# The first norm's modulation in a two-layer hybrid backbone: float32 weights kept in TensorE, two conditions moved past them, x loaded first

## The chip, the core and the metric

The kernel runs on one core of a Trainium2 chip. A core has five engines that run side by side: TensorE (matmuls, called PE in the profile; PEld is the load of its weights), VectorE (DVE), ScalarE (ACT), GpSimd (POOL) and SyncE (SP), which here issues most DMA transfers. Data stand in SBUF (128 partitions), matmul results in PSUM, inputs and outputs in HBM. TensorE has two clock levels, 1.2 and 2.4 GHz; the profile shows the granted clock as a share of the higher one (0.50 or 1.00). The metric is the device time of one launch in microseconds, the median of several runs.

## What is computed

Two layers of a diffusion backbone for 128 context tokens and 512 latent tokens, D = 1024. Each layer is a token mixer (layer 0: a gated short convolution; layer 1: a two-way state-space scan) followed by a product-key expert layer. All of it is float32. What the change touches is the first norm of layer 0, with a shift and a scale that come from a condition vector, one for the context (`c_ctx`) and one for the latents (`c`):

```python
def run_trunk(x, cond, ...):
    for i in range(DEPTH):
        mod = (jax.nn.silu(cond) @ ada_w[i] + ada_b[i])[:, None, :]
        sh_a, scl_a, gt_a, sh_f, scl_f, gt_f = jnp.split(mod, 6, axis=-1)
        hn = rmsnorm(x, norm_mix_g[i]) * (1 + scl_a) + sh_a
        mix = short_conv_mixer(hn, ...)          # layer 0
        x = x + gt_a * mix
        ...

def short_conv_mixer(h, w_in, conv_w, w_out, grid):
    bg, cg, xv = jnp.split(h @ w_in, 3, axis=-1)
    return (bg * dwconv3(cg * xv, conv_w, grid)) @ w_out
```

`sh_a` and `scl_a` are the first 2048 of the 6144 columns of `silu(cond) @ ada_w[0]`. Only these are needed before the first projection.

## The kernel before

Activations lie with channels on the partitions: x is 8 tiles (k = 0..7) of 128 channels by 640 tokens (512 latent, 128 context). A float32 product of the large kind is done in three matmuls of a faster format: each operand is split into a high part (a copy on ScalarE, `Stream.high` L89 or `split` L120) and the rest (a subtraction on VectorE, L98 or L121), and `mm3` (L123 to L127) adds high x high, high x low and low x high.

The first 70 us of the program go through these stages.

- `run` (L143) loads the small vectors, makes `sl` = silu(cond) for both conditions (128 x 8 x 2) and splits it into `silu` (four columns per k).
- `ada` (L220) computes the shift and the scale. Its 16 weight tiles of 0.52 MB come through a `Stream` (tag "a": raw `ar`, high `ah`, low `al`). Here the condition is the stationary operand (four columns, a high and a low one per condition) and the weights move past it, 512 columns a matmul, into `arow` (L232, L233). A row of four results is copied to `arows` (L237), and four small float32 matmuls against `sel` (L242) add high and low and turn the row into columns, in `apm`; ScalarE copies them to `mod` (L243), and `modulated` (L269) adds the bias and makes `gs` = (1 + scale) times the norm's weight. This is done for four parts of 512 columns. `ada` is a generator; `conv_layer` steps it at fixed places among the other instructions.
- x is loaded on the same SP queue, after the first five `ar` tiles (L412).
- `stat` (L283) squares each tile of x on ScalarE (`sq`), adds them up on VectorE, and matmuls with `ones` give the sums `st` (L294). `rstd` (L310) turns these into the norm's factor `rs`, with five transposes `rb` (L319).
- `norm` (L322) makes for each k: `nt` = x * rs on VectorE (L327), times `gs` plus shift on ScalarE for each of the two token groups (L329), and the split into `chi` and `clo` (L120, L121).
- The conv layer's loop over j (8 channel tiles of each of the three projections): `cg`, `xv` and `bg`, each 48 matmuls of 320 columns (16 of `mm3`'s triples). For j = 0 `cg` and `xv` run with `rows=True`: k is the outer loop, so a k is used as soon as its tile is there. Their weights come through the stream `win` (raw `wr`, high `wh`, low `wl`). Beside the loop VectorE computes the other modulation parts (`modulation`, L247), two multiply-and-sum steps for each 128 columns.

The order within an engine is set by a scheduler of the language, which sorts the instructions by its own model of time from the order in the code; only the expert layers have an order written out by hand. Each engine then takes its instructions strictly in that order and waits where an operand isn't there. Tiles with a name and `bufs=n` share n buffers in turn.

Of the kernel before, what the change touches and what calls it, by code (L numbers as in the profile page):

```python
# [9 lines left out]
F32 = mybir.dt.float32  # L10
F32R = mybir.dt.float32r
# [4 lines left out]
AF = mybir.ActivationFunctionType  # L16
ALU = mybir.AluOpType
# [4 lines left out]
P = 128  # L22
NL = 512
# [4 lines left out]
KT = 8  # L28
D = 1024
# [12 lines left out]
START = 4  # L42
# [71 lines left out]
class K:  # L114
# [28 lines left out]
    def run(s):  # L143
        nc, A = s.nc, s.A
        with ExitStack() as ctx:
# [24 lines left out]
            s.silu = c.tile([P, KT, 4], F32R, name="silu")  # L170
            for n in range(2):
                s.split(s.silu[:, :, 2 * n], s.silu[:, :, 2 * n + 1], sl[:, :, n])
            s.sel = c.tile([4, 2], F32, name="sel")
            nc.sync.dma_start(s.sel, A["sel"])
# [45 lines left out]
    def ada(s, parts, pool, ps, loads=3):  # L220

        nc = s.nc
        st = Stream(s, pool, [s.A["ada_w"][n, q] for _, n in parts for q in range(4)], "a", loads, 2)
        st.prime()
        for e, (i, n) in enumerate(parts):
            row = ps.tile([P, 512], F32, name="arow", tag="arow", bufs=1)[:4]
            for q in range(4):
                wh, wl = (t.rearrange("p a b -> p (a b)").rearrange("p (a b) -> p a b", a=2)
                          for t in st.get(4 * e + q))
                for k in range(2):  # L230
                    c = s.silu[:, 2 * q + k, :]
                    nc.tensor.matmul(row, c, wh[:, k, :], start=(q + k == 0), stop=False)  # L232
                    nc.tensor.matmul(row, c, wl[:, k, :], start=False, stop=(q + k == 4))  # L233
                if q < 3:
                    yield True
            r = pool.tile([4, 512], F32, name="arows", bufs=2)
            nc.scalar.activation(r, row, AF.Copy)  # L237
            yield True
            yield True
            pm = ps.tile([P, NL], F32, name="apm", tag="apm", bufs=1)[:, :8].rearrange("p (a b) -> p a b", b=2)  # L240
            for m in range(4):
                nc.tensor.matmul(pm[:, m, :], r[:, m * P:(m + 1) * P], s.sel, start=True, stop=True)  # L242
            nc.scalar.activation(s.mod[i][:, 4 * n:4 * n + 4], pm, AF.Copy)  # L243
            s.modulated(i, n)
            yield True
# [148 lines left out]
    def conv_layer(s):  # L394
        nc, A = s.nc, s.A
        with ExitStack() as ctx:
            big = s.pool(ctx, "cbig")
            tmp = s.pool(ctx, "ctmp", bufs=2)
            win = Stream(s, s.W, [A["sc_w_in"][m] for m in range(24)], "w")
            wout = Stream(s, s.W, [A["sc_w_out"][m] for m in range(8)], "w")  # L400
            hi = big.tile([P, KT, NT], F32R, name="chi")
            lo = big.tile([P, KT, NT], F32R, name="clo")
# [4 lines left out]
            ps = s.pool(ctx, "cps", space=PSUM)  # L407
            ax = ExitStack()
            mods = s.ada([(0, n) for n in (2, 0, 3, 1)], s.pool(ax, "cada"), ps, START)
            next(mods)  # L410
            for k in range(KT):
                nc.sync.dma_start(s.x[:, k, :], A["xT"][:, k, :])  # L412
            for _ in range(11):
                next(mods)
# [4 lines left out]
            with ExitStack() as nx:  # L419
                tp = s.pool(nx, "normtmp")  # L420
                for _ in mods:
                    pass
                win.prime()
                s.norm(0, 0, hi, lo, tp)
# [947 lines left out]
def lay(I):  # L1372
# [4 lines left out]
    A = {}  # L1377

    def mt(w):

        k, n = w.shape[0] // P, w.shape[1] // P
        return np.ascontiguousarray(w.reshape(k, P, n, P).transpose(2, 1, 0, 3).reshape(n, P, k * P))
# [6 lines left out]
    def col(v):  # L1389
# [11 lines left out]
    A["ada_w"] = np.ascontiguousarray(  # L1401
        w[0, :, :2048].reshape(4, 2, P, 4, 512).transpose(3, 0, 2, 1, 4)).reshape(4, 4, P, D)
    A["ada_wT"] = np.ascontiguousarray(w.transpose(0, 2, 1)).reshape(2, 48, P, D)
    A["sel"] = np.repeat(np.eye(2, dtype=np.float32), 2, axis=0)
# [46 lines left out]
```

## Time and profile before

| | |
|---|---|
| median of 3 runs | 4118.25 us (4109.04 to 4119.88) |
| profiled execution | 4117.18 us, its span 4115.5 us |
| TensorE busy | 4000.5 us (97% of the span) |
| VectorE busy | 3414.4 us (83%) |
| ScalarE busy | 1661.4 us (40%) |
| mean granted clock | 0.987 |

The span is what the profiler sees from the first to the last instruction; the execution's time has 1.7 us more around it. Busy shares are means over stages of very different kind: the first 50 us, which the change touches, are one eightieth of the span, and there TensorE has gaps and a lower clock. So the rows to read are those of the stage, not of the whole. A matmul's duration in a row is longer than its distance from the next, since matmuls are pipelined; prices of matmuls in a row are taken from the distances. "[idle before <-releaser]" at a row's end tells how long the engine had waited and for whom.

### The profile page before, as it was taken

Reading aid. Unit: us, or ns where it says so; the run is one execution under the profiler, and the core shown is the slowest. Engines: PE = TensorE matmul, PEld = TensorE weight load, DVE = VectorE, ACT = ScalarE, POOL = GpSimd, SP = SyncE. Lnnn points to the kernel's source line nnn. Section 1 sums busy time; section 2 is a strip of 40 time slices with the busy share of each in tenths; the row PEclk is TensorE's granted clock in tenths of the full one; section 3 lists DMA queues with packets and bytes.
Section 4 is the critical chain, followed back from the end, with each engine's and each line's share of the span. In section 5 each row is a group of like instructions: output and inputs, shape, how many; then the busy total and the mean of one; then the engine's idle time right before and its main releaser. Section 6 shows DMA issues by size and latency. Waiting matters only on the chain.

```text
span 4115.5 us, 59000 instructions
## 1 busy us (share of the span) xinstructions
PE 4000.5 (97%) x22253; PEld 3543.9 (86%) x22253; DVE 3414.4 (83%) x6324; ACT 1661.4 (40%) x3060; POOL 421.6 (10%) x535
## 2 busy tenths in 40 slices
PE   8999999999999999999999999999999999999998
PEld 6999978788888888888999998987878888888887
DVE  7979997678788888878999867998858878888886
ACT  5233234433333333336555644223443333333332
POOL 0000000001111111111010100000001111111110
PEclk8999999999999999999999999999999999999999
DMA  6643238888888888963333234224888889998894
GB/s 218 219 159 109 81 131 248 266 307 321 313 316 324 322 322 322 327 249 123 118 102 119 85 128 148 94 86 161 249 280 300 323 316 325 323 323 321 323 324 181
DMA packets 344807, 957.33 MB, mean 233 GB/s; under 512 B 30091, under 2 KB 192139, under 8 KB 302537
## 3 DMA queue, kind: packets, MB, share of 16 engines
q1 hardware_dynamic: 147914, 514.53, 36.5%
q0 software_dynamic: 52224, 338.36, 22.1%
q10 hardware_dynamic: 144384, 100.67, 7.7%
q8 instruction: 174, 2.85, 0.3%
q14 instruction: 111, 0.91, 0.1%
HBM read 839.34 MB, written 114.04 MB: 232 GB/s over the span
## 4 chain that ended last, share of the span: by engine, by line
issue 41%; PE 32%; DVE 14%; POOL 8%; ACT 2%; DMA 2%; ACTq 1%; POOLq 0%; SPq 0%; DVEq 0%
POOL uv L587 8%; PE pact L125 3%; PE pact L126 3%; PE pact L127 3%; PE pj L125 2%; PE pj L126 2%; PE pj L127 2%; DVE ul L98 1%; DVE wl L98 1%; PE pg L978 1%; DMA uv<-uv,cidx 1%; PE pg L979 1%; DVE pr L825 1%; DVE idx L799 1%; DVE scr L795 1%
## 5 line engine op out<-in xcount | busy, mean ns | idle before, releaser
L125 PE MATMUL pact<-hnh,uh 128*128 128x480 f32 x2048 | 789.7, 386 | 12.7 <-ACT ga L508 9.4
L127 PE MATMUL pact<-hnh,ul 128*128 128x480 f32 x2048 | 781.7, 382 | 9.6 <-DVE ul L98 9.4
L126 PE MATMUL pact<-hnl,uh 128*128 128x480 f32 x2048 | 784.1, 383 | 0.0
L125 PE MATMUL acc<-h,wh 128*128 128x480 f32 x1536 | 584.6, 381 | 0.0
L127 PE MATMUL acc<-h,wl 128*128 128x480 f32 x1536 | 581.7, 379 | 0.0
L126 PE MATMUL acc<-h,wh 128*128 128x480 f32 x1536 | 581.7, 379 | 0.0
L89 ACT ACTIVATE wh<-wr 128x1024 fp32r<-128x1024 f32 x385 | 404.8, 1052 | 398.1 <-DMA wr<-uv 105.1
L98 DVE TENSOR_TENSOR wl<-wr,wh 128x1024 fp32r<-128x1024 f32 x385 | 469.7, 1220 | 59.4 <-ACT wh L89 58.3
L587 POOL DMA_INDIRECT uv<-uv,cidx x320 | 335.7, 1049 | 1661.8 <-DVE cacc L604 1540.1
L125 PEld LDWEIGHTS pact<-hnh,uh 128*128 128x128 f32 x2048 | 387.0, 189 | 76.1 <-ACT ga L508 13.1
L127 PEld LDWEIGHTS pact<-hnh,ul 128*128 128x128 f32 x2048 | 386.5, 189 | 74.0 <-DVE ul L98 13.6
L594 DVE SCALAR_TENSOR_TENSOR uv<-uv,hrow 128x1024 f32<-128x1024 f32 x320 | 390.8, 1221 | 57.3 <-DMA uv<-uv,cidx 55.6
L126 PEld LDWEIGHTS pact<-hnl,uh 128*128 128x128 f32 x2048 | 386.5, 189 | 58.3
L604 DVE SCALAR_TENSOR_TENSOR cacc<-uv,dg,cacc 128x1024 f32<-128x1024 f32 x316 | 405.1, 1282 | 0.0
L508 ACT ACTIVATE ga<-pact 128x480 f32<-128x480 f32 x256 | 145.6, 569 | 626.3 <-PE pact L127 626.0
L98 DVE TENSOR_TENSOR ul<-ur,uh 128x1024 fp32r<-128x1024 f32 x256 | 312.3, 1220 | 88.7 <-ACT uh L89 88.2
L89 ACT ACTIVATE uh<-ur 128x1024 fp32r<-128x1024 f32 x256 | 269.0, 1052 | 252.5 <-DMA ur<-uT 111.2
L581 DVE TENSOR_TENSOR h<-h,h 128x480 fp32r<-128x480 f32 x256 | 168.5, 658 | 197.0 <-PE rot L126 196.5
L127 PEld LDWEIGHTS acc<-h,wl 128*128 128x128 f32 x1536 | 289.1, 188 | 46.1
L126 PEld LDWEIGHTS acc<-h,wh 128*128 128x128 f32 x1536 | 289.1, 188 | 44.1
L125 PEld LDWEIGHTS acc<-h,wh 128*128 128x128 f32 x1536 | 289.4, 188 | 43.1
L596 ACT ACTIVATE dg<-dg 128x1 f32<-128x1 f32 x320 | 63.9, 200 | 422.3 <-DVE uv L594 422.3
(342 smaller groups left out, 8004.8 us busy)
## 6 DMA issues: line engine op xcount, KB each, us to landing
ur<-uT SPq DMA_DIRECT2D x256, 512.0 KB
wr<-uv SPq DMA_DIRECT2D x256, 512.0 KB
gdram<-st ACTq DMA_DIRECT2D x30, 2048.0 KB
gt<-gdram SPq DMA_DIRECT2D x62, 960.0 KB
mw<-ada_wT SPq DMA_DIRECT2D x80, 512.0 KB
adram<-ga ACTq DMA_DIRECT2D x128, 240.0 KB
ga<-adram SPq DMA_DIRECT2D x128, 240.0 KB
wr<-ssd_w SPq DMA_DIRECT2D x48, 512.0 KB
```

The source lines that it names most:

```text
L89: s.K.nc.scalar.activation(hi.rearrange("p a b -> p (a b)"), s.raw[s.nh], AF.Copy)
L98: s.K.nc.vector.tensor_sub(lo.rearrange("p a b -> p (a b)"), s.raw.pop(s.ns), hi.rearrange("p a b -> p (a b)").bitcast(F32))
L125: mm(out, wh, mh, start=start, stop=False)
L126: mm(out, wh, ml, start=False, stop=False)
L127: mm(out, wl, mh, start=False, stop=stop)
L508: nc.scalar.activation(g, pa, AF.Gelu)
L581: nc.vector.tensor_sub(h2, h, h1.bitcast(F32))
L587: nc.gpsimd.indirect_dma_start(out=t[:], out_offset=None, in_=A["uv"].rearrange("l e d -> (l e) d"), in_offset=bass.IndirectOffsetOnAxis(a ...
L594: nc.vector.scalar_tensor_tensor(UV[n][:, :D], UV[n][:, :D], 1.0, rows[n >= NX], op0=ALU.mult, op1=ALU.mult, accum_out=dg[:, n:n + 1])
L596: nc.scalar.activation(dg[:, n:n + 1], dg[:, n:n + 1], AF.Gelu)
L604: nc.vector.scalar_tensor_tensor(cacc, t[:, D:], dg[:, n:n + 1], cacc, op0=ALU.mult, op1=ALU.add)
L795: nc.vector.match_replace(scr[:, t], v[:, t, :8], src[:, t], imm_value=-3e38)
```

## The change

The weights of the first 2048 columns are laid out like other weights, 16 tiles of 128 columns with all eight k-parts in each. They stay float32 and unsplit, and now they are the stationary operand: for each 128 columns, eight matmuls with a 128 x 128 piece in the array and the two columns of `sl` moving past it, straight into columns of `apm`. `sel`, `silu`, `arow` and `arows` are gone. For each k the shift (tile k) and the scale (tile 8 + k) are done together (`first_mod`), followed by the norm of that k alone. x is loaded ahead of all weight tiles; these have six buffers, three pairs. The stream `win` is started in the turn of k = 4.

```diff
-    def ada(s, parts, pool, ps, loads=3):
+    def first_load(s, k, pool):
+        out = []
+        for m in (k, KT + k):
+            w = pool.tile([P, KT, P], F32, name="aw", bufs=AHEAD)
+            s.nc.sync.dma_start(w.rearrange("p a b -> p (a b)"), s.A["ada_w"][m])
+            out.append(w)
+        return out
+
+    def first_mod(s, k, ws, ps):
         nc = s.nc
...
-                    nc.tensor.matmul(row, c, wh[:, k, :], start=(q + k == 0), stop=False)
-                    nc.tensor.matmul(row, c, wl[:, k, :], start=False, stop=(q + k == 4))
...
+        pm = ps.tile([P, NL], F32, name="apm", tag="apm", bufs=1)[:, :4].rearrange("p (a b) -> p a b", b=2)
+        for a, w in enumerate(ws):
+            for q in range(KT):
+                nc.tensor.matmul(pm[:, a, :], w[:, q, :], s.sl[:, q, :], start=(q == 0), stop=(q == KT - 1))
+        for a in range(2):
+            m = KT * a + k
+            nc.vector.tensor_add(s.mod[0][:, m], pm[:, a], s.sv("adab", 2, 48)[:, 0, m:m + 1].to_broadcast([P, 2]))
+        nc.vector.scalar_tensor_tensor(s.gs[0][:, 0, k], s.mod[0][:, KT + k], 1.0,
+                                       s.sv("nmg", 2, KT)[:, 0, k:k + 1].to_broadcast([P, 2]),
+                                       op0=ALU.add, op1=ALU.mult)
...
-            mods = s.ada([(0, n) for n in (2, 0, 3, 1)], s.pool(ax, "cada"), ps, START)
-            next(mods)
+            ap = s.pool(ax, "cada")
             for k in range(KT):
                 nc.sync.dma_start(s.x[:, k, :], A["xT"][:, k, :])
-            for _ in range(11):
-                next(mods)
+            aw = {k: s.first_load(k, ap) for k in range(AHEAD // 2)}
...
                 tp = s.pool(nx, "normtmp")
-                for _ in mods:
-                    pass
-                win.prime()
-                s.norm(0, 0, hi, lo, tp)
+                for k in range(KT):
+                    s.first_mod(k, aw.pop(k), ps)
+                    if k + AHEAD // 2 < KT:
+                        aw[k + AHEAD // 2] = s.first_load(k + AHEAD // 2, ap)
+                    if k == 4:
+                        win.prime()
+                    s.norm(0, 0, hi, lo, tp, ks=[k])
```

AHEAD is 6. What this does to the order on the engines is seen at three places. On TensorE, from the last transpose of `rb` on, the order before has the last modulation part and then the first projections; `cg_472` and `cg_473` are the two halves of the tokens, and so `xv_536` and `xv_537`:

```order
L233 MATMUL arow<-al,silu 4x512
L125 MATMUL cg_472<-chi,wh 128x320
L125 MATMUL cg_473<-chi,wh 128x320
L126 MATMUL cg_472<-clo,wh 128x320
L127 MATMUL cg_472<-chi,wl 128x320
L126 MATMUL cg_473<-clo,wh 128x320
L127 MATMUL cg_473<-chi,wl 128x320
L242 MATMUL apm<-sel,arows 128x2 x4
L125 MATMUL xv_536<-chi,wh 128x320
L126 MATMUL xv_536<-clo,wh 128x320
```

The program's first matmuls on TensorE now, up to the same place (L230 is the new modulation matmul, L286 the sums, L311 the transposes of `rs`, L426 the later conditions' rows):

```order
L230 MATMUL apm<-sl,aw 128x2 x16
L286 MATMUL st<-ones,sq 128x64 x10
L230 MATMUL apm<-sl,aw 128x2 x16
L311 MATMUL rb<-ident,rt 128x128 x4
L230 MATMUL apm<-sl,aw 128x2 x8
L311 MATMUL rb<-ident,rt 128x128
L426 MATMUL srow<-ident,sl 128x128 x4
L230 MATMUL apm<-sl,aw 128x2 x88
L426 MATMUL srow<-ident,sl 128x128 x4
L125 MATMUL cg_455<-chi,wh 128x320
L126 MATMUL cg_455<-clo,wh 128x320
L125 MATMUL cg_456<-chi,wh 128x320
```

Before, the projections of the first k stand ahead of the last modulation part's turn into columns, and `xv` follows at once, mixed with `cg`; now all 128 modulation matmuls stand ahead of the first `cg`, and all of `cg` ahead of `xv`. On ScalarE, the copy `wh` of the first projection's weights stood ahead of the first scaled `nt`:

```order
L237 ACTIVATE arows<-arow 4x512
L89 ACTIVATE wh<-wr 128x1024
L243 ACTIVATE mod_92<-apm 128x8
L89 ACTIVATE ah<-ar 128x1024
L329 ACTIVATE nt<-nt,mod_92,gs_94 128x512
L89 ACTIVATE ah<-ar 128x1024
L329 ACTIVATE nt<-nt,mod_92,gs_94 128x128
```

and at the end of the norm there is now, on ScalarE:

```order
L321 ACTIVATE nt<-nt,mod_85,gs_87 128x128
L120 ACTIVATE chi<-nt 128x640
L427 ACTIVATE silurow<-srow 128x512
L321 ACTIVATE nt<-nt,mod_85,gs_87 128x512
L89 ACTIVATE wh<-wr 128x1024
L321 ACTIVATE nt<-nt,mod_85,gs_87 128x128
L427 ACTIVATE silurow<-srow 128x512
L120 ACTIVATE chi<-nt 128x640
```

The first `wh` has moved from ahead of the first `nt` to behind the first half of the last one (the last `chi` is the eighth). On SP the loads start so before:

```order
L158 DMA sm<-small 128x306
L160 DMA cnd<-condT 128x16
L174 DMA sel<-sel 4x2
L81 DMA ar<-ada_w 128x1024 x5
L412 DMA x<-xT 128x640 x8
L81 DMA ar<-ada_w 128x1024 x9
```

and now, on the same queue:

```order
L158 DMA sm<-small 128x306
L160 DMA cnd<-condT 128x16
L403 DMA x<-xT 128x640 x8
L220 DMA aw<-ada_w 128x1024 x16
L81 DMA wr<-sc_w_in 128x1024 x2
```

x has moved ahead of all modulation weights, and the first projection's weights `wr` behind all of them. On every engine the order is the same as before from within the conv layer's loop to the end of the program.

## Rows read from the trace of the kernel before

**Rows 1.** Busy time by stretches: columns are named in the first line.

```profile
core 0: us, PE busy (x) PEld busy (x) DVE busy (x) ACT busy (x) POOL busy (x), PEclk, DMA share, GB/s
68.00:281.00 213.00, 212.77 (x1452) 212.32 (x1452) 193.75 (x337) 54.58 (x69) 1.55 (x32) 1.00 0.60 195
```

**Rows 2.** Timeline of TensorE, end of `xv`, start of `bg`: start us, us, what.

```profile
67.37 0.31 PE L127 MATMUL xv<-chi,wl 128*128 128x320 f32 x1
67.52 0.31 PE L125 MATMUL bg<-chi,wh 128*128 128x320 f32 x1
```

**Rows 3.** Chain of waits in order of time, 43 to 52 us: start us, us, what.

```profile
43.40 1.22 DVE al L98
...
46.63 0.80 ACT nt L329
...
48.41 1.23 DVE al L98
49.63 0.74 DVE nt L327
50.37 0.75 DVE clo L121
```

**Rows 4.** Timeline of weight loads with few moving columns; xN merges N records.

```profile
27.69 3.32 PEld L294 LDWEIGHTS st<-ones,sq 128*128 128x128 f32 x14 [0.30 <-issue]
...
33.67 1.78 PEld L242 LDWEIGHTS apm<-sel,arows 4*128 4x128 f32 x8 [0.64 <-ACT arows L237]
...
43.79 0.96 PEld L242 LDWEIGHTS apm<-sel,arows 4*128 4x128 f32 x8 [1.31 <-ACT arows L237]
...
282.39 1.19 PEld L294 LDWEIGHTS st<-ones,sq 128*128 128x128 f32 x10 [1.89 <-ACT sq L289]
```

**Rows 5.** The tile `apm`: min/median/max ns of its weight loads, first and last start.

```profile
L242 PEld LDWEIGHTS apm<-sel,arows x32: 181/187/333, 15.1 to 52.7; 4*128 4x128 f32 x32
```

**Rows 6.** Busy time by stretches, 24 to 44 us, columns as in rows 1.

```profile
24.00:40.00 16.00, 15.13 (x52) 9.64 (x53) 7.76 (x10) 8.92 (x12) 0.00 (x0) 0.50 0.60 197
40.00:44.00 4.00, 2.93 (x15) 1.29 (x13) 3.53 (x4) 3.59 (x6) 0.00 (x0) 0.97 0.76 245
```

**Rows 7.** Busy time by stretches, the first 15 us, columns as in rows 1.

```profile
0.00:5.00 5.00, 0.00 (x0) 0.00 (x0) 1.88 (x7) 1.81 (x4) 0.70 (x6) 1.00 0.48 118
5.00:10.00 5.00, 2.19 (x5) 0.51 (x6) 2.45 (x2) 2.67 (x3) 0.00 (x0) 1.00 0.93 365
10.00:15.00 5.00, 4.29 (x12) 0.89 (x10) 3.50 (x3) 3.69 (x6) 0.00 (x0) 1.00 0.98 346
```

**Rows 8.** Timeline, the first modulation tile: issued on SP, taken by ScalarE.

```profile
2.15 6.54 SPq L81 DMA_DIRECT2D ar<-ada_w  x5
...
6.03 1.06 ACT L89 ACTIVATE ah<-ar 128x1024 fp32r<-128x1024 f32 x1 [2.25 <-DMA ar<-ada_w]
```

**Rows 9.** Timeline of ScalarE, two squares of x in a row.

```profile
18.17 0.74 ACT L289 ACTIVATE sq<-x 128x640 f32<-128x640 f32 x1 [0.89 <-DVE sq L301]
...
19.80 0.74 ACT L289 ACTIVATE sq<-x 128x640 f32<-128x640 f32 x1 [0.89 <-DVE sq L301]
```

**Rows 10.** Timeline, the steps from modulation to the first projection.

```profile
35.78 0.17 DVE L273 TENSOR_TENSOR mod<-mod,sm 128x8 f32<-128x8 f32 x1 [0.36 <-ACT mod L243]
...
43.64 1.04 ACT L89 ACTIVATE wh<-wr 128x1024 fp32r<-128x1024 f32 x1
...
45.35 1.22 DVE L98 TENSOR_TENSOR wl<-wr,wh 128x1024 fp32r<-128x1024 f32 x1
```

**Rows 11.** Timeline of TensorE, wide matmuls in a row after a pause.

```profile
2458.78 1.42 PE L125 MATMUL pj<-yhi,wh 128*128 128x320 f32 x4
...
2461.06 0.47 PE L127 MATMUL pj<-yhi,wl 128*128 128x320 f32 x1
2461.33 0.47 PE L125 MATMUL pj<-yhi,wh 128*128 128x320 f32 x1
...
2463.89 0.31 PE L126 MATMUL pj<-ylo,wh 128*128 128x320 f32 x1
```

More of the change, by code (lines that the diff above doesn't have):

```diff
@@ L41 @@
 GATHER = (0.62, 1.95)
-START = 4
+AHEAD = 6
 MORE = (1, 1, 0, 4)
@@ L169, in run @@
             nc.scalar.activation(sl, cnd, AF.Silu)
[L170 to L174, printed above, removed]
             s.mod = [c.tile([P, 48, 2], F32, name=f"mod{i}") for i in range(2)]
@@ L217, in final @@
                 nc.sync.dma_start(s.A["yT"][:, k, :], o)
-    def ada(s, parts, pool, ps, loads=3):
-        nc = s.nc
[L223 to L231, printed above, removed]
-                    nc.tensor.matmul(row, c, wh[:, k, :], start=(q + k == 0), stop=False)
-                    nc.tensor.matmul(row, c, wl[:, k, :], start=False, stop=(q + k == 4))
[L234 to L245, printed above, removed]
@@ L1399, in lay @@
     w = f("ada_w")
-    A["ada_w"] = np.ascontiguousarray(
-        w[0, :, :2048].reshape(4, 2, P, 4, 512).transpose(3, 0, 2, 1, 4)).reshape(4, 4, P, D)
+    A["ada_w"] = mt(w[0, :, :2048])
     A["ada_wT"] = np.ascontiguousarray(w.transpose(0, 2, 1)).reshape(2, 48, P, D)
-    A["sel"] = np.repeat(np.eye(2, dtype=np.float32), 2, axis=0)
     w = mt(f("sc_w_in")[0]).reshape(3, 8, P, D)
```

## The prediction

> **What bounds the kernel now.** I read the page's busy shares first, then the busy time of each engine by stretches, then the chain of waits, and then single rows of the first 70 us in the timeline. Between 68 and 281 us TensorE is busy 212.77 of 213.00 us [rows 1]: from the first `bg` projection to the end of the conv layer's second product nothing but TensorE's own work sets the time. TensorE gets into that stretch at 67.52 us, where the last `xv` product of the first channel tile gives way to `bg` [rows 2]. Moving that moment moves everything behind it. There is no slack to take a delay up, since TensorE waits only 0.23 us in 213. So the question is a single one: when does the first `bg` matmul start.
>
> What sets it today is the modulation. The chain of waits runs, before the first projection, through the split of the modulation weights (`ah`, `al`), the first scaled tile `nt`, another split that stands before it on both engines, and then `clo` [rows 3]. From there on the norm's tiles and TensorE's `cg` and `xv` go side by side: the two products of j = 0 are written in rows of k so that each k is used as soon as its tile is normed, and both end soon after the last `clo`.
>
> **What is taken out.** 16 splits on ScalarE and 16 on VectorE, 64 wide matmuls on `arow`, the four copies `arows` and the four groups on `sel`. This frees much of ScalarE and VectorE before 50 us, and x no longer queues behind five modulation loads on SP. None of it counts by itself after 68 us; it counts only as far as the first `bg` comes earlier.
>
> **What is put in.** 128 matmuls of full float32, each with 128 columns of weights in the array and two columns moving. The order shows that four such matmuls on `apm` (before) are eight records in the trace, a pair per matmul [rows 4]; so 128 are 256 records, all on TensorE, in one row, and by the new order all of them stand ahead of the first `cg` matmul. That last point is the step I rest on: the norm goes tile by tile, but the 88 last modulation matmuls are issued before any projection, so `cg` and `xv` no longer run beside the norm. They come after it. What stood side by side now stands in a row.
>
> The price of a record. With the clock at 2.4 GHz, eight take 0.96 us, less the last one's own 0.19: (0.96 - 0.19) / 7 = 0.110 us each; the ten on `st` at 282 us give (1.19 - 0.19) / 9 = 0.111. With the clock at 1.2 GHz, (1.78 - 0.33) / 7 = 0.207 us, and on `st` (3.32 - 0.33) / 13 = 0.230 [rows 4]; a record's own length is 0.19 or 0.33 [rows 5]. The number of moving columns (2 or 64) changes little; the weights' 128 columns are paid in full each time. The new form is not in the trace, but it has two moving columns as `apm` has and 128 rows of weights as `st` has, so I keep 0.111 and 0.230 as the ends. No gain is possible here, since each record is work on the engine that everybody waits for.
>
> Which clock. From 24 to 40 us TensorE is busy 15.13 of 16 us and the granted clock is 0.50 throughout; it rises only in the stretch from 40 us, after wide `arow` matmuls in a row [rows 6]. In those 16 us lie the 14 narrow records on `st` and the eight on `apm`, both without a gap between them. So narrow matmuls in a row, busy by the records, did not bring the clock up. The new stream is narrower still, and TensorE has idled some 13 us ahead of it. I take 1.2 GHz for all 256 records, at 0.207 us, the row with two moving columns: 256 x 0.207 = 53.0 us.
>
> The Trainium skill reads otherwise in one place: "TensorE: Matmul & The Clock Gate", section "What's actually happening", says that activity releases the throttle, which for a stream without gaps means 2.4 GHz soon after its start; the trace does not agree for its narrow records, and this is the first rival below. The same page, "LDWEIGHTS (loading the stationary operand)", gives 128 / 1.2 = 107 ns for such a load, an estimate of 27 us for 256 of them; the rows at 2.4 GHz agree (0.110), those at 1.2 GHz do not (0.207). By the page the sum below would come out 26 us lower.
>
> When the stream starts. SP now issues x (8 x 0.33 MB) before the 16 weight tiles (0.52 MB each). Ahead of the end of the first tile there are 0.16 + 2.62 + 0.52 = 3.30 MB. The rates of the first three stretches moved 0.59, 1.82 and 1.73 MB [rows 7], so 3.30 MB are through at 12.6 us. A landing is seen about 0.75 us after that reckoning: 0.68 MB would be through at 5.25 us, and ScalarE could use the first tile at 6.03 [rows 8]. Start: 13.4 us. The second tile is needed 3.3 us later and lands at 14.9; later pairs wait for freed buffers (six), 1.05 MB per 6.6 us, which takes 2.9 us at 365 GB/s.
>
> The statistics don't delay it. Square and sum go at 1.63 us a tile [rows 9], from x's first landing near 5.3 us (0.49 MB, by the same reckoning), so the last square is done near 17 us, while TensorE is on the first 32 new records until 20.0. The `st` records come behind those. The norm's scale `rs` is ready near 36 us and no tile but the first three could use it sooner, so loading x first buys nothing that the end sees.
>
> **The sum to the end of the stream.** 13.4 start; 53.0 for 256 records; 20 on `st` x 0.230 = 4.6; five on `rb` and the first four on `srow` x 0.230 = 2.1; and the wait for `apm`. That tile has one buffer: tile k + 1 may not begin before VectorE has read tile k. Price: the last record's tail 0.16, two small adds of 0.17 each [rows 10] and the hand-over, some 0.6 us; for the first two tiles other work of TensorE covers it, five are left: 3.0. Together 76.1 us.
>
> **From there to `bg`.** Two adds and `gs` 0.75, first half of the last `nt` 0.80 [rows 3], `wh` 1.04, `wl` 1.22 [rows 10], hand-overs 0.2: 4.0 us. By the new order ScalarE does `wh` of the first projection only behind the last tile's `nt`, so this is all in a row, before the first matmul on `wl`; four of the 96 `cg` and `xv` matmuls lie within it. The other 92 at 0.147 (1452 records in 213 us, [rows 1]) are 13.5 us, four `srow` 0.9. And the clock is low at their start: in a like place later, wide matmuls start at 2458.78 and run at 0.27 us until just before 2463.89 [rows 11], 5 us. In 5 us at 0.267 go 19 matmuls in place of 34: 15 x 0.147 = 2.2 us lost. 76.1 + 4.0 + 13.5 + 0.9 + 2.2 = 96.7 us, against 67.5. The change costs **29 us**.
>
> Where this could be given back: VectorE runs six more modulation steps in the j = 0 stretch than before, but it is not the bound behind it. From the first channel tiles on, all engines have the same order as before to the end of the program, so the shift is carried along unchanged. The profiled execution took 4117.2 us (span 4115.5 and 1.7 around it), 1.1 under the median of 4118.25. 4117.2 + 29.2 = 4146.4 for a profiled one, 4147 for a median.
>
> **The rivals.** (a) Not slower: the clock comes up during the stream. At 0.111 us from the first record on, the 256 take 28.4, `st` 2.2, the other nine 1.0; 13.4 + 28.4 + 2.2 + 1.0 + 3.0 = 48.0, and with 4.0 + 13.5 + 0.4 the first `bg` is at 65.9, 1.6 us earlier than now. With the first pair of tiles still at 1.2 GHz (32 x 0.096) it is at 69.0: 4120 us. It decides from where some two thirds of the records run at 2.4 GHz. For it: there is no gap between the records. Against: 24 to 40 us [rows 6]. This is where the skill's sentence on activity would lead. (b) A longer row: VectorE's adds queue behind the norm's `nt` and `clo`, some 0.75 each [rows 3], so that the wait for `apm` is 2 us, and a record costs 0.230: 7 + 5.9 us more, 4160. For it: VectorE takes its instructions in turn, and a `clo` waits for ScalarE. Against: the adds of two tiles come 6.6 us apart, and the norm's two steps fill 1.5 us of that. (c) Faster by over 12 us: `bg` would have to start by 55 us, though 48.0 is reached with every record at 2.4 GHz and 18 us follow. I see no row for it.
>
> **How the numbers follow.** Forecast (+29) 0.74, (b) 0.11, (a) 0.13, (c) 0.02. About 0.3%, or 12 us, is what a measurement of this kernel tells from no change: slower by more holds the forecast and (b), 0.85; within it (a), 0.13; faster 0.02. The range reaches down from 4147 by the waits for `apm` (3), the clock's loss (2) and a start 2 us sooner, and by 9 for the scatter of the runs before: 4131. Up: (b) and 2 of scatter, 4162. Only (a), (c) and a tail of (b) are left out.
>
> **What would show it.** In the profile after: the `apm` records as one group of 256, 0.2 us apart, with the clock at 0.50 from about 13 to 80 us; no `cg` matmul before the last of them; `wh` behind the last `nt` on ScalarE; `bg` first near 97 us; then TensorE full for 213 us again. If the clock reads 1.00 in the stream, (a) holds and the step on narrow matmuls was wrong. If `cg` starts while `apm` records remain, the order misled me. If `bg` is late but the end is not, there was slack that I missed.

## The result, and the profile after

The changed kernel takes 4150.92 us (median of 6 runs, 4147.02 to 4155.67); the kernel before, beside it, 4117.01 (6 runs, 4109.04 to 4122.51). The ratio is 1.0085, 95% interval 1.0072 to 1.0099: some 34 us slower. The profiled execution took 4155.66 us, its span 4154.0. On the page of after TensorE is busy longer, and VectorE and ScalarE less:

```profile
PE 4039.3 (97%) x22413; PEld 3595.1 (87%) x22413; DVE 3395.8 (82%) x6324; ACT 1644.4 (40%) x3034; POOL 421.8 (10%) x535
```

39 us more on TensorE in this pair of profiles (36 between the means of three profiles of after and two of before), 19 less on VectorE, 17 less on ScalarE: work went from two engines with room to the one that is busy 97% of the span. Where it stands is in the timeline of TensorE (start us, us, what; in brackets the idle time ahead and who ended it):

```profile
13.46 6.96 PE L230 MATMUL apm<-sl,aw 128*128 128x2 f32 x32 [13.46 <-DMA aw<-ada_w]
20.28 4.51 PE L286 MATMUL st<-ones,sq 128*128 128x64 f32 x20
24.58 6.93 PE L230 MATMUL apm<-sl,aw 128*128 128x2 f32 x32
32.22 1.09 PE L311 MATMUL rb<-ident,rt 128*128 128x128 f32 x4 [0.71 <-DVE rt L307]
33.10 3.41 PE L230 MATMUL apm<-sl,aw 128*128 128x2 f32 x16
...
41.83 6.99 PE L230 MATMUL apm<-sl,aw 128*128 128x2 f32 x32 [0.32 <-DVE mod L233]
49.14 6.99 PE L230 MATMUL apm<-sl,aw 128*128 128x2 f32 x32 [0.32 <-DVE mod L233]
...
71.06 6.99 PE L230 MATMUL apm<-sl,aw 128*128 128x2 f32 x32 [0.32 <-DVE mod L233]
77.91 1.09 PE L426 MATMUL srow<-ident,sl 128*128 128x128 f32 x4
80.36 0.63 PE L125 MATMUL cg<-chi,wh 128*128 128x320 f32 x1 [1.35 <-ACT wh L89]
80.79 0.47 PE L126 MATMUL cg<-clo,wh 128*128 128x320 f32 x1
81.05 0.47 PE L125 MATMUL cg<-chi,wh 128*128 128x320 f32 x1
...
97.95 0.31 PE L127 MATMUL xv<-chi,wl 128*128 128x320 f32 x1
98.10 0.31 PE L125 MATMUL bg<-chi,wh 128*128 128x320 f32 x1
```

The last two lines answer to [rows 2]: the first `bg` starts at 98.10 us in place of 67.52, 30.6 later. From 13.46 to 78.05 there is one long row of modulation records, 32 for each k (its shift tile and its scale tile together, called a tile from here on), and from the fourth tile on TensorE waits in it for 0.32 us a tile. 32 records last 6.99 us, less the last one's own 0.35: 6.64 / 31 = 0.214 us each. The tile `apm` (min, median, max ns of one; first and last start), for [rows 5]:

```profile
L230 PEld LDWEIGHTS apm<-sl,aw x256: 288/333/338, 13.4 to 77.6; 128*128 128x128 f32 x128
```

Behind it stands the chain of waits (start us, us, what), in place of [rows 3]:

```profile
71.06 7.00 PE apm L230 x32
78.08 0.24 DVE mod L233 x2
78.34 0.17 DVE gs L235
78.54 0.81 ACT nt L321
79.36 0.96 ACT wh L89
80.36 0.63 PE cg L125
```

These are the modulation of the last tile, two adds, `gs`, the first half of the last `nt`, and only then `wh`, as the order has it. Further behind, by stretches (columns as in [rows 1]):

```profile
24.00:40.00 16.00, 14.93 (x71) 14.57 (x70) 2.05 (x6) 3.11 (x7) 0.00 (x0) 1.00 0.31 99
98.10:311.10 213.00, 212.66 (x1452) 212.22 (x1450) 186.48 (x325) 54.10 (x68) 1.55 (x32) 1.00 0.59 186
```

TensorE is as good as full again in the 213 us from the first `bg`. From there to the transfer that closes the conv layer it is 213.4 us, and before 214.0: what is late at 98 us is late at the layer's end.

The first of these lines sets a trap. Its granted clock reads 1.00 from 24 to 40 us, where [rows 6] had 0.50, and it does so all through the stream. But 0.214 us a record is the price at 1.2 GHz [rows 4], and behind the stream the `cg` matmuls stand 0.267 us apart (80.79, 81.05) until 85.4 us and 0.147 apart from 86.4. The first change of the clock in this trace is a rise, at 86.2 us; ahead of it the trace has no value, and the column shows 1.00, which is not a reading. One of the runs below (a warm start) has changes on record from 5.2 us on, and there the column shows 0.50 with the same distances. [rows 7] has the same: 1.00 between 5 and 10 us, while `arow` matmuls of 512 columns in that stretch stood 0.43 us apart, against 0.23 at 45 us.

### The profile page after: what moved, and what is told of

It reads as the page before. It is cut to its first block, busy times and chain, and to the rows that moved or that the text cites. A ratio compares the mean times of both kernels' runs of the same rounds, so it can differ in the third digit from the quotient of the medians.

```text
span 4154.0 us, 59280 instructions
## 1 busy us (share of the span) xinstructions
PE 4039.3 (97%) x22413; PEld 3595.1 (87%) x22413; DVE 3395.8 (82%) x6324; ACT 1644.4 (40%) x3034; POOL 421.8 (10%) x535
## 4 chain that ended last, share of the span: by engine, by line
issue 40%; PE 32%; DVE 14%; POOL 8%; DMA 3%; ACT 2%; ACTq 1%; POOLq 0%; SPq 0%; DVEq 0%
POOL uv L580 8%; PE pact L125 3%; PE pact L126 3%; PE pact L127 3%; PE pj L126 2%; PE pj L125 2%; PE pj L127 2%; PE apm L230 1%; DVE wl L98 1%; DVE ul L98 1%; PE pg L971 1%; DMA uv<-uv,cidx 1%; PE pg L972 1%; DVE idx L792 1%; DVE scr L788 1%
```

## The experiments

"Conv end" is the start of the transfer that closes the conv layer, in one profile: 281.5 us before, 311.5 after. It is given as its distance to 281.5. The second profile of before has 279.7 and the other two of after 310.7 and 310.6, so 1 or 2 us between two profiles decide nothing. Ratios are against the kernel before on the same chip.

**Again.** The changed kernel, unchanged, beside the first three experiments.

> The changed kernel once more, with no edit, for a second profile and a narrower interval. Theory (all of the loss is in the first 100 us, +30.0 us at every milestone of the conv layer, and what the first profile shows beyond it, 38.5 at the end, is the scatter of the later stages): bg first near 98 us again, the rest of the span (from the first bg to the end) between 4045 and 4060 us and not the 4056 of the first profile to a microsecond, ratio 1.0073 (30 of 4117). Rival (the later stages are slower too, by some 8 us): the rest is again near 4056, against 4048 in the kernel before, and the ratio is 1.009 or more.

Measured: 4150.01 us, ratio 1.0081 (1.0068 to 1.0095), `bg` at 97.25 us. The result repeats. From the first `bg` to the end it is 4052.5 us, and the ratio lies between the theory's and the rival's: what happens behind the first 100 us is not decided by this run.

**Half of the records.**

```diff
-            for q in range(KT):
-                nc.tensor.matmul(pm[:, a, :], w[:, q, :], s.sl[:, q, :], start=(q == 0), stop=(q == KT - 1))
+            for q in range(0, KT, 2):
+                nc.tensor.matmul(pm[:, a, :], w[:, q, :], s.sl[:, q, :], start=(q == 0), stop=(q == KT - 2))
```

> Only the even half of the contraction is done (64 matmuls in place of 128), with all loads, adds, norms and the same order; the odd half of the modulation is left out, so this is a price and not a version. Theory (256 records of 0.21 us in a row are the cost): 128 records and 27 us less, bg first at 71 us, total near 4124. Rival (the serial order, projections behind the norm, or the loads, or the waits on apm set the end): the stream gets shorter but bg moves by less than 10 us, total over 4140.

Measured: 4123.13 us, ratio 1.0016 (1.0006 to 1.0025), conv end +1.9, `bg` at 69.94 us. TensorE's timeline:

```profile
42.91 3.57 PE L230 MATMUL apm<-sl,aw 128*128 128x2 f32 x16 [0.32 <-DVE mod L233]
46.80 3.58 PE L230 MATMUL apm<-sl,aw 128*128 128x2 f32 x16 [0.32 <-DVE mod L233]
50.23 1.09 PE L426 MATMUL srow<-ident,sl 128*128 128x128 f32 x4
52.68 0.64 PE L125 MATMUL cg<-chi,wh 128*128 128x320 f32 x1 [1.35 <-ACT wh L89]
```

The waits, the order and the way from the stream to `bg` are those of after; a tile takes 3.90 us in place of 7.31. 128 records fewer take 28.2 us off, 0.22 each. The cost goes with the number of records.

**Projections beside the stream.** The order of the norm's loop written out by hand: `cg` and `xv` of a k behind the modulation of the next k, and the projections' weights started at k = 0.

```diff
+                order.enter_context(s.tc.manual_schedule())
...
-                for k in range(KT):
+                for k in range(KT + 1):
...
-                    if k == 4:
+                    if k == 0:
                         win.prime()
...
+                    else:
+                        for g in gens:
+                            next(g), next(g)
```

> The changed kernel with the order of the norm's loop written out by hand: the projections' weights are started in the turn of k = 0, and the cg and xv matmuls of a k stand behind the modulation of the next k, among the modulation's records, where the changed kernel has them behind all of them (some of the first bg move there too, so the end of the conv layer, 281 us before and 311 after, is the moment to read). Theory (the stream of records keeps TensorE full at 1.2 GHz, and work put beside it is added to it): what stands beside the stream takes its time out of it, at 0.267 us a matmul where the clock is low; the conv layer ends between 2 us earlier and 8 us later than in the changed kernel, the total is 4146 to 4158. If the wide matmuls raise the clock, the stream is shortened too: 10 to 25 us earlier, 4125 to 4140, and a record's distance in the trace is then near 0.11. Rival (what costs is that norm and projections stand in a row, some 14 us): the conv layer ends 10 to 14 us earlier with the records still 0.215 us apart, total 4136 to 4140.

Measured: 4148.52 us, ratio 1.0072 (1.0056 to 1.0088), conv end +32.2, which is 2 to 3 us later than in the three profiles of after. TensorE:

```profile
42.48 0.47 PE L125 MATMUL bg<-chi,wh 128*128 128x320 f32 x1
42.75 6.82 PE L230 MATMUL apm<-sl,aw 128*128 128x2 f32 x32
49.43 0.61 PE L126 MATMUL bg<-clo,wh 128*128 128x320 f32 x1
...
53.31 0.47 PE L127 MATMUL xv<-chi,wl 128*128 128x320 f32 x1
53.58 3.86 PE L230 MATMUL apm<-sl,aw 128*128 128x2 f32 x32
57.29 0.48 PE L126 MATMUL bg<-clo,wh 128*128 128x320 f32 x1
57.57 0.47 PE L127 MATMUL bg<-chi,wl 128*128 128x320 f32 x1
```

The rival that norm and projections in a row are what costs has fallen: its 10 to 14 us did not come. Side by side is no better, since TensorE is nearly full either way and most of the projections are now paid at 0.267. The rows tell more. The tile at 42.75 takes 6.68 us to the next start, 0.209 a record; the one at 53.58, behind 15 wide matmuls, takes 3.71, 0.116 a record. It is the same instruction on the same kind of tile in one kernel: the price of a record follows the clock. And the clock doesn't stay: the trace has it up from 54.04 us and down from 57.46, and behind those 32 records the projections stand 0.27 apart again. Two more of the eight tiles ran for the most part at 2.4 GHz in the same way, so the run mixes two things, a cheaper stream and dearer projections; the run with half of the records, in the order of after, is the cleaner test.

**A warm start.** 36 matmuls of zeros, 512 columns wide, in TensorE's idle time ahead of the stream.

```diff
+            for _ in range(36):
+                nc.tensor.matmul(wo, wv[:, :P], wv[:, P:P + 512], start=True, stop=True)
```

> 36 wide matmuls of zeros (512 columns) in the time in which TensorE waits for the first weight tile, into a PSUM bank that nothing reads; nothing else is changed. Theory (a narrow record costs 0.21 us at 1.2 GHz and 0.11 at 2.4, and narrow records in a row do not hold the clock up): the clock is at 2.4 GHz when the stream starts at 13.5 us, the first 30 to 60 of the 256 records go at 0.11, then the clock falls and the rest go at 0.21; bg first at 92 to 95 us, total 3 to 6 us below the changed kernel, near 4146. Rival (the stream was slow only because it began at the low clock, and would hold the high one): all 256 at 0.11, bg first near 71 us, total near 4124. Second rival (0.21 is the price of the new form at either clock): no change at all.

Measured: 4148.19 us, ratio 1.0081 (1.0069 to 1.0093), conv end +27.8, `bg` at 95.93 us, 1.3 to 2.2 us earlier than in the three profiles of after.

```profile
13.35 5.09 PE L230 MATMUL apm<-sl,aw 128*128 128x2 f32 x32 [1.95 <-DMA aw<-ada_w]
18.30 4.51 PE L286 MATMUL st<-ones,sq 128*128 128x64 f32 x20
22.60 6.93 PE L230 MATMUL apm<-sl,aw 128*128 128x2 f32 x32
```

The granted clock from 15.5 us to the stream's end (columns as in [rows 1]):

```profile
15.50:75.60 60.10, 57.70 (x267) 56.92 (x268) 14.61 (x38) 16.86 (x27) 0.00 (x0) 0.50 0.43 142
```

The first 32 records take 5.09 us, where 6.96 is the price at 1.2 GHz and some 3.9 (as in the run above) that at 2.4: the clock fell among them, at 15.4 us, and it did not come back in the 57 us to the stream's end. So here 0.50 and 6.93 us for 32 records stand side by side. `bg` moved the way that was forecast, but not to 92 to 95 us, and the total shows no gain: the ratio, 1.0081, is that of the unchanged kernel beside it.

**Wide matmuls among the records.** One of those matmuls of zeros behind every four records, the order of the loop by hand.

```diff
+                if q % 2:
+                    nc.tensor.matmul(hold, wv[:, :P], wv[:, P:P + 512], start=True, stop=True)
...
+                nx.enter_context(s.tc.manual_schedule())
```

> The changed kernel with 64 wide matmuls that are of no use (bf16, 512 columns of zeros into a PSUM tile that nobody reads), one behind every two of the modulation's matmuls, and the order of the norm's loop written out by hand so that they stand there. With that order the first wh also comes ahead of the last norm tiles, some 2.3 us off the path. Theory (the price of the stream is the low clock, and the clock is low because the stream's own matmuls are narrow): the clock comes up within the first two tiles and stays up; a record falls from 0.215 to about 0.111 us, so 256 of them go from 55 to some 30 us, and 64 wide ones of 0.21 to 0.32 us put back 13.6 to 20; the projections behind need no rise of the clock (2.2 us). The first bg comes at 78 to 88 us in place of 98, the total is 4131 to 4142. Rival (the records are slow for a reason of their own, such as the loading of float32 weights, whatever the clock): a record stays near 0.21 us, the 64 wide ones come on top, the first bg comes at 108 to 116 us and the total is 4160 to 4170. Rival (the clock is not raised by wide work of this share): the wide ones at 1.2 GHz are 0.43 us each, bg comes near 122, total 4172.

Measured: 4154.12 us, ratio 1.0086 (1.0071 to 1.0101), conv end +32.6, `bg` at 100.7 us. Early and late in the stream:

```profile
14.49 0.85 PE L231 MATMUL apm<-sl,aw 128*128 128x2 f32 x4
15.20 0.59 PE L233 MATMUL hold<-pad 128*128 128x512 bf16 x1
15.58 0.85 PE L231 MATMUL apm<-sl,aw 128*128 128x2 f32 x4
...
81.90 0.50 PE L231 MATMUL apm<-sl,aw 128*128 128x2 f32 x4
82.26 0.38 PE L233 MATMUL hold<-pad 128*128 128x512 bf16 x1
82.47 0.50 PE L231 MATMUL apm<-sl,aw 128*128 128x2 f32 x4
```

Four records and a wide one take 1.09 us in the first six tiles: the clock stays low, and no forecast of a rise there held. Between the sixth and the seventh tile 30 of the projections stand in a row; among them the clock comes up (0.267 apart until 77 us, 0.147 behind), and the last two tiles run at 2.4 GHz: 0.36 us for four records in place of 0.71, 0.57 with the wide one. So the second rival, records that are slow at either clock, falls. My theory's price was, if anything, too high (by its terms 0.65 to 0.76 for such a group), and its way of getting there was wrong. The third rival, the clock that this mix does not raise, holds for six tiles of eight. Its 4172 was not reached because the two fast tiles save 8 us (16 x 0.515), and because a wide matmul adds only 0.23 us to four records (1.09 less 4 x 0.214) where the rival had 0.43, 10 us over six tiles.

**Both, and both with an early start.** First 42 matmuls of zeros ahead and the wide ones among the records (edits as above). Then 12 ahead, x behind the first six weight tiles, projection weights at k = 2 and the norm three turns behind the modulation:

```diff
+            aw = {k: s.first_load(k, ap) for k in range(AHEAD // 2)}
             for k in range(KT):
                 nc.sync.dma_start(s.x[:, k, :], A["xT"][:, k, :])
...
+                    if k >= LAG:
+                        s.norm(0, 0, hi, lo, tp, ks=[k - LAG])
```

> The kernel with 64 wide matmuls of zeros among the modulation's records, and 42 more of them in TensorE's idle time ahead of the stream. Alone, the 42 ahead (36 there) did not keep the clock up, and the 64 among the records did not bring it up; but there the last two tiles, behind wide projections that had brought it up, ran at 2.4 GHz to their end: four records and one wide matmul took 0.575 us, where the tiles before took 1.09. Theory (a share of wide work that cannot raise the clock holds it once it is up): eight tiles take 8 x 4.6 = 37 us in place of 64 (to 91 us there), with st, rb and srow the stream ends near 56 to 62 us, the conv layer ends 5 us later to 3 us earlier than in the kernel before, the total is 4113 to 4126. Rival (the clock falls all the same, at st's 20 narrow records or sooner): the stream runs at 1.09 us per four records from there on, it ends at 75 to 91 us, the conv layer ends 15 to 32 us later than before, the total is 4133 to 4154.

> The same with 12 wide matmuls of zeros ahead of the stream (that idle time ends near 5.6 us here), x loaded behind the first six weight tiles, the projections' weights started in the turn of k = 2, and the norm of a k three turns behind its modulation, so that VectorE does not hold the modulation up while it waits for rs. Theory (record price at 2.4 GHz plus an early start): the stream ends at 46 to 54 us, the conv layer ends 0 to 10 us earlier than in the kernel before (281.5 us), the total is 4107 to 4117. Rival (the clock falls in the stream): the conv layer ends 10 to 25 us later than before, the total is 4127 to 4145.

Measured: 4159.65 us, ratio 1.0098 (1.0083 to 1.0113), conv end +32.6 for the first; 4153.45 us, ratio 1.0090 (1.0077 to 1.0104), conv end +32.7 for the second. Both theories fell, and both kernels came later than their rivals' ranges too (up to 4154 and 4145). In the first:

```profile
15.63 0.58 PE L231 MATMUL apm<-sl,aw 128*128 128x2 f32 x4
16.07 0.59 PE L233 MATMUL hold<-pad 128*128 128x512 bf16 x1
16.45 0.85 PE L231 MATMUL apm<-sl,aw 128*128 128x2 f32 x4
```

The clock is up when the stream starts at 13.25 and down from 16.07 on; in the second kernel from 14.20 on, 7 us into its stream. So the two fast tiles of the run above, and the last two of the first kernel here, do not show that such a mix holds the clock. The second kernel has two late tiles of that kind as well: behind wide projections they run at 2.4 GHz from 72.5 us, with 13 wide projections between them, and the clock falls at 82.4, within the second of them. The second kernel also made a wait of its own: TensorE stood 4.78 us for the sums of the squares, which VectorE did behind the adds of the first tiles, and so its early start was lost.

**x behind the first weights.**

```diff
+            aw = {k: s.first_load(k, ap) for k in range(AHEAD // 2)}
             for k in range(KT):
                 nc.sync.dma_start(s.x[:, k, :], A["xT"][:, k, :])
-            aw = {k: s.first_load(k, ap) for k in range(AHEAD // 2)}
```

> One part undone: the eight loads of x stand behind the first six weight tiles on SP instead of ahead of all. Theory (TensorE's stream of narrow records sets the end, so what counts is when it starts, and x first only delays it): the stream starts at 6 us in place of 13.4, its end and the first bg come 7.4 us earlier (bg at 90.7), total near 4143; the norm's factor is later but still early enough. Rival (loading x first helps, since the norm needs x and its factor before anything can be scaled): bg not earlier or later than 98, total 4151 or more.

Measured: 4145.15 us, ratio 1.0076 (1.0061 to 1.0091), conv end +25.6, `bg` at 93.73 us.

```profile
5.62 6.96 PE L230 MATMUL apm<-sl,aw 128*128 128x2 f32 x32 [5.62 <-DMA aw<-ada_w]
...
36.58 4.53 PE L286 MATMUL st<-ones,sq 128*128 128x64 f32 x20 [2.08 <-DVE sq L293]
...
66.21 6.98 PE L230 MATMUL apm<-sl,aw 128*128 128x2 f32 x32 [1.07 <-DVE mod L233]
```

The stream starts 7.8 us earlier, and 4.4 of them arrive at `bg`; 2.1 go into a wait for the squares, 0.75 into a longer wait for `apm`, and some into the steps behind. With x first, the order of the loads costs the changed kernel some 4 us at `bg` (3.5 to 4.4 by the three profiles of after), and the rest of the 30 stays. The ratios of the totals (1.0076 here, 1.0081 for the unchanged kernel beside it) are too close to show so little.

**x in turns, in the kernel before.** The loads of x and the squares between the modulation's tiles.

```diff
+            st = ps.tile([P, CH, SW], F32, name="st", tag="bg0", bufs=1)
             for k in range(KT):
                 nc.sync.dma_start(s.x[:, k, :], A["xT"][:, k, :])
-            for _ in range(11):
                 next(mods)
...
                 s.stat(k, tmp, st, k < KT - 1, tag="cgs")
+                next(mods)
```

> The kernel before with the loads of x taking turns with the modulation's weight tiles in the code, so that squares and splits alternate one to one on ScalarE where the squares stood in a row; modulation itself as before. Theory (before, TensorE waits 5.48 us at 17 to 23 us for splits that stand behind squares, and the stage's end follows from the modulation's progress): the first bg comes 3 to 8 us earlier than 67.5, the total is 4109 to 4114. Rival (the stage is set by TensorE's own work at 1.2 GHz from 24 to 40 us, which the gap does not shorten): bg within 2 us of 67.5, total 4114 to 4118.

Measured: 4116.57 us, ratio 0.9993 (0.9984 to 1.0003), conv end +1.7, `bg` at 69.73 us. The gap of 5.48 us in TensorE's row is gone, and no gain is shown: `bg` is 2.2 us later, just outside the rival's 2, and not 3 to 8 earlier. The `arow` matmuls run at 1.2 GHz from 26.5 to 47 us, 0.43 apart, and the first projections from 50.4 to 57 us, where in the first profile of before the clock was up from 40 on. That the edit did this is not shown. The second profile of before, the same kernel unchanged (the run is given below), has other times again: up at 29.9 us, down at 33.3, up at 36.7, down at 43.6, up at 47.0, and `bg` at 65.68, 1.8 us earlier than in the first. For [rows 6] it gives:

```profile
24.00:40.00 16.00, 14.14 (x60) 8.25 (x61) 9.25 (x11) 10.26 (x14) 0.00 (x0) 0.71 0.66 211
```

So the theory, an earlier `bg`, fell; the rival, that this stage is set by TensorE's own work at the low clock, fits, and one profile can't show more. I found no kernel that is faster than the one before.

**What is lost behind the conv layer.** In the first profile of after, 7.9 us of the 38.5 arise behind the first `bg`, where the order is the same. One kernel puts the removed constants back, so that later tiles lie where they lay:

```diff
+            s.silu = c.tile([P, KT, 4], F32R, name="silu")
...
+            s.sel = c.tile([4, 2], F32, name="sel")
+            nc.sync.dma_start(s.sel, A["sel"])
```

> The changed kernel with the two constant tiles that the change removed put back, unused: silu with its four small splits and sel with its load. The later tiles then lie at the addresses that they had before. Theory (the 4 to 5 us that the changed kernel loses behind the conv layer, on top of the 30 us ahead of it, come from where its later tiles lie): the first bg at 98 us as in the changed kernel, 4 to 5 us fewer behind it, total 4145 to 4146. Rival (the loss is one of when things start, or the runs' scatter): the same loss behind the conv layer, total 4149 to 4152.

Measured: 4151.68 us, ratio 1.0077 (1.0063 to 1.0091), conv end +29.2, the end of the span +33.9: 4.7 us arise behind the conv layer with the old layout too, so the layout does not explain them. Then both kernels once more, unchanged:

> The kernel before, unchanged, as one of the compared kernels, for a second profile of it. What is open is whether the changed kernel loses some 4 to 8 us behind the conv layer too: its two profiles have 4055.9 and 4052.5 us from the first bg to the end of the span, the one profile of before 4048.0. Theory (that is the runs' scatter): this profile's stretch lies between 4049 and 4056 us and the median's ratio to the other runs of before is within 0.1% of 1. Rival (the stretch belongs to the kernel): 4048 again within 1 us, the median within 0.1% all the same.

> The changed kernel, unchanged, on the same chip as the second profile of before. Theory (scatter): the stretch from the first bg to the end lies between 4048 and 4056 us, the median is 29 to 33 us over before's. Rival (the stretch belongs to the kernel): 4052 to 4056 us, the median 34 to 36 us over before's.

Measured: 4115.82 us (ratio 0.9994, 0.9985 to 1.0003) and 4150.95 us (1.0078, 1.0064 to 1.0092). From the first `bg` to the end of the span it is 4048.0 and 4046.5 us in the two profiles of before, 4055.9, 4052.5 and 4045.6 in three of after. One profile of after is below both of before: a loss that belongs to the kernel isn't shown, and profiles of one kernel differ by 10 us there. Mean `bg` is 97.5 us (98.10, 97.25, 97.20) against 66.6 (67.52, 65.68), 30.9 us; the medians of the three pairs differ by 33.9, 34.6 and 33.0. The last 2 to 4 us of that have no place that I can name. In the run with wide matmuls ahead and among the records, as much as 10 us arise behind the conv layer, in the median too (42.5 against 32.6); why is open.

## Why the prediction held, step by step

Predicted were 4147 us and a first `bg` at 96.7; measured are 4150.9 and 98.1. The change cost 33.9 us where 29.2 were forecast: 1.7 of the difference stand ahead of `bg` (30.9 by the means), and 3.0 are the ones behind it that have no place. The sum, term by term:

| term | predicted, us | in the profile of after, us |
|---|---|---|
| start of the stream | 13.4 | 13.46 |
| 256 records | 53.0 (0.207 each) | 54.8 (0.214 each) |
| `st` | 4.6 | 4.3 (20.28 to 24.58) |
| `rb`, first `srow` | 2.1 | 2.2, and waits of 0.71 and 0.37 beside them |
| five waits for `apm` | 3.0 | 2.3 (7.31 a tile, less 32 x 0.214) |
| end of the stream | 76.1 | 78.05 |
| to the first matmul on `wl` | 4.0 | 4.24 |
| from there to `bg` | 16.6 | 15.8 |
| first `bg` | 96.7 | 98.10 |

- **The record's price** was taken at its lower end, from the row with two moving columns; the measured one lies between the ends (0.207, 0.230), a third of the way up. This is the largest miss of the sum, 1.8 us. The waits for `rt` and `rs`, 1.1 us, had no term. The waits for `apm`, `st` and the last stretch were put too high, 1.8 us together, so that the sum came out closer than its terms.
- **The clock.** The step that carried most, 1.2 GHz for all 256 records, held, and rival (a) did not come: in no run did the records alone bring the clock up or keep it. Its condition, two thirds of the records at 2.4 GHz, was not met even with wide work put in. The row it was read from [rows 6] carries less than the prediction put on it: it is one execution's, and in the second profile of before the clock comes up at 29.9 us, among the 14 narrow records on `st`. That 1.2 GHz held for the new stream is shown by its own profiles and by the warm start. The sentence of the Trainium skill that stood behind it ("TensorE: Matmul & The Clock Gate", "What's actually happening", activity releases the throttle) does not describe this stream, 64 us with gaps of 0.3 to 0.7 us only. The figure of its section "LDWEIGHTS (loading the stationary operand)", 107 ns, is near the price at 2.4 GHz (0.116) and half of that at 1.2 (0.209 to 0.214).
- **The marker for it failed as I had written it**: "if the clock reads 1.00 in the stream, (a) holds". It reads 1.00, and (a) doesn't hold. Distances between starts were the right marker, and the text had used them for its prices.
- **Side by side and in a row.** I said that I rest on the order, `cg` and `xv` behind the norm in place of beside it. The order is as told, but it isn't what costs: beside each other they are no faster, and with half of the records, in the same order, 28 us are gone. What costs is that TensorE was given 55 us of records at the low clock and was relieved of less, 64 `arow` matmuls (an estimate from their distances, 0.23 to 0.43 us: 15 to 27 us); the sum had this right, the words around it did not.
- **x first** "buys nothing that the end sees": true, and too mild. It holds the stream back by 7.8 us and costs some 4 at `bg`. The prediction counted the late start in its 13.4 and never asked what it would be otherwise.
- **`wh` behind the last `nt`** and the rise of the clock behind it came as told, 4.2 us and until 86.2.
- **The rest of the program** carries the delay along, as forecast. Rival (b) named two causes of a longer row: its wait of 2 us did not come (0.46), its record price came by a third.

## What to carry to other kernels

Price a step by what it puts on the engine that sets the time, at the clock which that engine has there: moving work off VectorE and ScalarE, which had room, onto TensorE, which sets the time, lost 30 us. A float32 matmul with 128 columns of weights and two moving ones cost two records of 0.21 us at 1.2 GHz, nearly what 64 moving columns cost (0.230 by [rows 4]); where a few columns meet a large matrix, the form in which the matrix moves past them was the cheaper one here. And check a clock column against distances between starts before a conclusion rests on it.

## What the runs showed of the hardware

- A stream of narrow float32 records ran 64 us at 1.2 GHz, nearly without gaps, and a clock that wide matmuls had brought up fell within its first 32 records (at 15.4 us, 2 us into it). I had expected this of the stream, but not that one wide matmul behind every four records would neither raise the clock (60 us at 1.09 us a group) nor keep it where it was up (down from 16.07 and from 14.20 us). It stayed up for the last two such tiles in two kernels, with 13 wide projections between them, and in a third it fell within the second of the two.
- A record's price nearly halves with the clock: 0.209 and 0.116 us in one kernel, 0.71 and 0.36 for four in another.
- The profile's granted clock reads 1.00 ahead of the first change on record, whatever the clock: in the profile of after for 86 us, of which the stream's 64 ran at 1.2 GHz.
- When the clock rises and falls in a stretch with mixed work is not the same in two executions of one kernel: up at 40.3 us in one profile of before; up at 29.9, 36.7 and 47.0 and down between in the other, with the first `bg` 1.8 us apart. So what an edit does to the clock there can't be read from one profile.
